# Whole 128x128 transposes for the half chunks of neighbourhood attention, in a one-core backbone step

## The chip, the cores and the metric

The kernel runs on one core of a Trainium2 chip. The metric is the device time of one execution in microseconds (us); the time of a kernel is the median of its runs.

## What is computed

One inference step of a hybrid backbone with one layer: 256 context tokens and 2048 latent tokens (a grid of 32 rows by 64 columns), 1024 wide, everything in float32. Each token is normalised and modulated, goes through one combined input projection into three mixers and their gates, and the mixers' outputs are merged, projected and added. What the change touches is the first mixer, attention with 8 heads of 64:

```python
s_loc = einsum(q_blk, k_band) * scale + bias      # latent: 8 x 16 neighbourhood, NEG_INF outside
s_ctx = einsum(q_blk, ctx_k) * scale              # and all 256 context keys
p = softmax(concatenate([s_loc, s_ctx], axis=-1), axis=-1)
o = einsum(p_loc, v_band) + einsum(p_ctx, ctx_v)
```

Context tokens attend to the 256 context keys alone. The other two mixers (a bidirectional gated linear recurrence and a short gated convolution) and the projections are untouched.

## The kernel before, in words

**Dense work and side work.** Most of the time goes into the input projection. `w_in_chunk` (lines 147 to 155) makes one tile of 128 output columns by 512 (or 256) tokens with 24 matmuls at line 153: each float32 operand is split into a high and a low part, and three products stand for one. Attention rides along: a generator (`Side`, line 181) is advanced by one or more units after each dense chunk, so that on TensorE units of attention stand between dense chunks. In the first attention stage (lines 819 to 824) one step goes with each dense chunk: first the prompt's 16 units, then the 32 units of latent group 0. In the second (lines 858 to 867) 101/27 steps, almost four, go with each of 28 dense chunks; these are the 96 units of the groups 1, 2 and 3.

**Groups, jobs, units.** The latent grid is cut into four groups of 8 rows, that is 512 queries (`GR`, line 697). A job is a group and a head; a unit is one of four blocks of 16 columns in it, 128 queries (8 rows by 16 columns) on the partitions. A unit's keys are 11, 15, 15 or 12 rows of 32 columns (352, 480, 480 or 384 keys) and the 256 context keys.

**One unit.** `attend1` (lines 575 to 599) computes scores on TensorE (line 583 against the context keys, line 587 against the neighbourhood, two products each) and the softmax on VectorE (DVE) and ScalarE (ACT): maximum at lines 588 and 590, negation at 595, exponential at 596, reciprocal at 597, scaling at 598. The result `p` has 128 query rows and up to 736 key columns. `attend2` (lines 601 to 616) transposes `p` in chunks of 128 keys, because the product with the values needs the keys on the partitions: line 611 on TensorE into PSUM banks `t`, then line 614 copies each bank to `pT` on ScalarE. `attend3` (lines 618 to 624) multiplies `pT` with the values, two units alternating, one in PSUM partitions 0 to 63 and one in 64 to 127. `advance` (line 635) keeps two units between `attend1` and `attend2`, and calls `attend3` for two units at a time (line 639), that is with every second unit.

**Half chunks.** A chunk holds 4 rows of keys. Some chunks lie within reach of only the upper or only the lower four query rows of the unit; lines 699 and 700 list for each group which chunk meets which queries. `(0, 0, 64)` says: chunk 0 for queries 0 to 63 alone. Groups 0 and 3 have one such half chunk in each unit, groups 1 and 2 have two, one for queries 0 to 63 and one for 64 to 127. Lines 777 to 779 spread the chunks of a unit, with the two chunks of context keys, over two banks: four whole chunks and one half for groups 0 and 3; three whole ones and a half, then one whole and a half, for groups 1 and 2. Before the change line 611 transposes of a half chunk only its 64 query rows, with the 64x64 corner of the identity; in the trace such a transpose has the shape `64*128 64x64`, a whole one `128*128 128x128`.

**Loads.** All of attention's loads are issued on GpSimd's (POOL's) queue: for each job the queries `qs` (line 728, 512 KB, both halves of the array hold a copy), the gate `sg` (line 734), for some the bias `bt` (line 731), for each new head its keys `kd` and `ck` (lines 715 and 717) and its values `vb` (line 722). The loads of the next job are issued after the first unit of a job (lines 785 to 788). `qs` has two buffers, so a load waits until the scores of the job two before have read theirs. POOL also computes the low parts of the weights (`wlo`, line 56). The dense weights `wraw` come on SP's queue.

Of the kernel before, what the change touches and what calls it, by code (L numbers as in the profile page):

```python
# [15 lines left out]
P = 128  # L16
# [28 lines left out]
def build(nc, tc, H):  # L45
    es = ExitStack()
    V, S, G, TE, SY = nc.vector, nc.scalar, nc.gpsimd, nc.tensor, nc.sync
# [46 lines left out]
    ident = cp.tile([P, P], F32, tag="ident", name="ident")  # L94
# [24 lines left out]
    def bank(name):  # L119
        return psA.tile([P, 512], F32, tag="bank", name=name, bufs=8)  # L120
# [115 lines left out]
    with tc.tile_pool(name="p0", bufs=2) as p0:  # L236
# [50 lines left out]
        w = p0.tile([P, 8], F32, tag="w", name="w", bufs=1)  # L287
# [313 lines left out]
    def attend2(nm, p, pv, oap):  # L601


        pT = AT[0].tile([P, 640], F32, tag="pT", name=f"pT{nm}", bufs=4)
        base, todo = 0, []
        for bi, part in enumerate(pv):
            tb = bank(f"t{bi}{nm}")
            off = 0
            for c0, v, keys, q0, q1 in part:
                w = q1 - q0  # L610
                TE.transpose(tb[:, off : off + w], p[q0:q1, c0 : c0 + P], ident[q0:q1, q0:q1])  # L611
                todo.append((oap(q0, q1), v[:keys], pT[:keys, base + off : base + off + w]))
                off += w
            S.copy(pT[:, base : base + off], tb[:, :off])  # L614
            base += off
        return todo

    def attend3(todos):

# [15 lines left out]
    def advance():  # L635
        if pend:
            old = pend.pop(0)
            tpd.append((attend2(*old[:4]), old[4]))
        if len(tpd) > 2 or (tpd and not pend):
            two = [tpd.pop(0) for _ in range(min(2, len(tpd)))]  # L640
            attend3([todo for todo, _ in two])
            for _, fin in two:
                if fin:
                    fin()
# [431 lines left out]
```

## Time and profile before

| what | value |
|---|---|
| time, median of 3 runs | 2610.14 us (2605.08 to 2614.53) |
| the profiled execution's own time | 2611.47 us |
| its span, first to last instruction | 2609.7 us |
| mean granted clock of TensorE (share of full speed) | 0.985 |
| TensorE matmuls busy | 2542.3 us (97%) |
| VectorE, ScalarE, GpSimd busy | 1104.2, 978.3, 876.7 us |
| instructions | 35312 |

How to read it: PE is TensorE's matmuls, PEld its weight loads, which overlap them; DVE is VectorE, ACT ScalarE, POOL GpSimd, SP the engine that issues most DMAs. An engine with a q behind it is its sequencer. L611 is line 611. A matmul is given as `out<-weights-side operands`, then the shape of the used array (rows*columns) and that of the moving operand; matmuls are pipelined, their ends are modelled and one starts before the last has ended. In a timeline a row is one or several instructions alike (x4): start in us from the span's beginning, duration in us, engine, line, operation, tiles, shape; in brackets the engine's idle time before it and what ended that. `issue` stands for idle time that no profiled event ended. In a group by shape the count is followed by busy us, the mean ns of one, and idle us before them. PEclk is the granted clock as a share of 2.4 GHz; a stretch is either at 1.0 (2.4 GHz) or at 0.5 (1.2 GHz), and other figures are means.

### The profile page before, as it was taken

The page shows a single profiled execution, that of the slowest core. Times are in us where ns is not written, and L with a number is a line of the kernel's source. Part 1 is how long each engine was busy: PE and PEld are TensorE (multiplying, and loading weights), DVE is VectorE, ACT ScalarE, POOL GpSimd, SP SyncE. Part 2 cuts the span into 40 slices and gives each one's busy share as a digit, 9 for nine tenths or more (in the row PEclk, how much of TensorE's full clock was granted, in tenths as well). Part 3 has the DMA queues.
Part 4 walks back from the last instruction along what each step waited for, and adds up shares of the span by engine and source line. Part 5 has one row for each costly group of instructions (what it writes and reads, how often), then busy time and mean ns, then how long its engine had stood idle before and what let it go on. Part 6 is the DMA issues. An engine that isn't in the chain of part 4 may idle for free.

```text
span 2609.7 us, 35312 instructions
## 1 busy us (share of the span) xinstructions
PE 2542.3 (97%) x13192; PEld 2077.4 (80%) x13192; DVE 1104.2 (42%) x2329; ACT 978.3 (37%) x1849; POOL 876.7 (34%) x757
## 2 busy tenths in 40 slices
PE   8999999999999999999999997999999999999998
PEld 4887788888878888888888886777777888888887
DVE  5101245555123331325777863455444134333433
ACT  4312443444223334436665653444444311111221
POOL 2311223323532321522544443233231413334642
PEclk9999999999999999999999998999899999999999
DMA  7335642332733434435642335455442466545442
GB/s 275 112 87 159 170 122 81 68 70 69 188 106 119 148 121 145 133 101 135 190 156 91 115 121 179 136 146 151 131 137 77 155 224 200 177 157 186 159 141 88
DMA packets 248812, 360.84 MB, mean 138 GB/s; under 512 B 88761, under 2 KB 124729, under 8 KB 247617
## 3 DMA queue, kind: packets, MB, share of 16 engines
q1 hardware_dynamic: 147360, 227.20, 28.7%
q0 software_dynamic: 47920, 64.26, 8.8%
q10 hardware_dynamic: 53360, 67.13, 7.8%
q8 instruction: 104, 1.70, 0.3%
q14 instruction: 68, 0.55, 0.1%
HBM read 248.10 MB, written 110.11 MB: 137 GB/s over the span
## 4 chain that ended last, share of the span: by engine, by line
PE 75%; DMA 6%; issue 4%; POOL 2%; DVE 1%; ACT 0%; SPq 0%; ACTq 0%; POOLq 0%; DVEq 0%
PE ps L153 45%; PE pb L932 12%; PE po L981 8%; DMA qs<-d_q 3%; PE t L611 3%; PE o L624 2%; PE pg L454 2%; PE pv L321 1%; PE sl L587 1%; PE sc L583 1%; DMA bt<-bias 1%; DMA d_z<-sp 1%; POOL wlo L56 0%; DMA kp<-d_k 0%; DMA d_q<-evl 0%
## 5 line engine op out<-in xcount | busy, mean ns | idle before, releaser
L153 PE MATMUL ps<-xh,whi 128*128 128x512 f32 (+1 forms) x2400 | 899.6, 375 | 0.0
L153 PE MATMUL ps<-xl,whi 128*128 128x512 f32 (+1 forms) x2400 | 888.8, 370 | 2.4 <-DVE xl L56 1.6
L153 PE MATMUL ps<-xh,wlo 128*128 128x512 f32 (+1 forms) x2400 | 888.2, 370 | 0.0
L153 PEld LDWEIGHTS ps<-xh,whi 128*128 128x128 f32 x2400 | 455.2, 190 | 93.7 <-issue 6.2
L56 POOL TENSOR_TENSOR wlo<-wraw,whi 128x512 fp32r<-128x512 f32 x240 | 334.0, 1409 | 570.0 <-ACT whi L55 505.3
L153 PEld LDWEIGHTS ps<-xh,wlo 128*128 128x128 f32 x2400 | 455.1, 190 | 78.1
L153 PEld LDWEIGHTS ps<-xl,whi 128*128 128x128 f32 x2400 | 455.2, 190 | 77.8 <-POOL xl L56 2.0
L55 ACT CAST whi<-wraw 128x512 fp32r<-128x512 f32 x240 | 144.8, 616 | 300.1 <-PE ps L153 160.9
L932 PE MATMUL pb<-zh,wbh 128*128 128x512 f32 (+1 forms) x480 | 179.0, 373 | 4.3 <-ACT zh L55 4.3
L167 ACT ACTIVATE evm<-ps 128x512 f32<-128x512 f32 (+1 forms) x120 | 66.3, 552 | 301.1 <-PE ps L153 300.2
L932 PE MATMUL pb<-zl,wbh 128*128 128x512 f32 (+1 forms) x480 | 179.1, 373 | 0.0
L932 PE MATMUL pb<-zh,wbl 128*128 128x512 f32 (+1 forms) x480 | 179.0, 373 | 0.0
L588 DVE TENSOR_SCALAR_CACHE_REDUCE p<-sc 128x256 f32<-128x256 f32 x127 | 53.9, 424 | 254.1 <-PE sc L583 253.1
L939 POOL TENSOR_TENSOR tg<-tg,tg 128x512 f32<-128x512 f32 (+1 forms) x80 | 96.9, 1221 | 188.5 <-DVE tg L935 184.3
L935 DVE SCALAR_TENSOR_TENSOR tg<-tg,pb 128x512 f32<-128x512 f32 (+1 forms) x120 | 74.7, 631 | 151.8 <-PE pb L932 139.8
L611 PE MATMUL t<-ident,p 128*128 128x128 f32 (+1 forms) x698 | 129.4, 286 | 7.0 <-DVE ast L595 3.4
L611 PEld LDWEIGHTS t<-ident,p 128*128 128x128 f32 (+1 forms) x698 | 91.6, 142 | 53.9 <-issue 19.6
L614 ACT COPY pT<-t 128x512 f32<-128x512 f32 (+3 forms) x256 | 96.2, 406 | 75.0 <-PE t L611 74.7
L596 ACT ACTIVATE p<-p,ast 128x736 f32<-128x736 f32 (+2 forms) x127 | 109.4, 862 | 39.5 <-DVE ast L595 38.1
L444 DVE SCALAR_TENSOR_TENSOR uf<-ut,pk,uf 128x512 f32<-128x512 f32 (+1 forms) x120 | 103.0, 858 | 30.5 <-ACT uf L441 28.6
L475 POOL TENSOR_TENSOR sq<-sq,ea 128x512 f32<-128x512 f32 (+1 forms) x40 | 61.9, 1548 | 154.2 <-ACT sq L468 92.6
L55 ACT CAST zh<-zr 128x512 fp32r<-128x512 f32 (+1 forms) x60 | 30.5, 575 | 211.8 <-PE pb L932 92.6
(233 smaller groups left out, 3689.7 us busy)
## 6 DMA issues: line engine op xcount, KB each, us to landing
wraw<-w_in SPq DMA_DIRECT2D x240, 256.0 KB, 3.4
d_sig<-evm ACTq DMA_DIRECT2D x96, 256.0 KB, 3.5
tg<-d_sig SPq DMA_DIRECT2D x96, 256.0 KB, 3.8
xt<-x SPq DMA_DIRECT2D x36, 512.0 KB, 3.7
qs<-d_q POOLq DMA_DIRECT2D x32, 512.0 KB, 17.1
zr<-d_z SPq DMA_DIRECT2D x12, 1024.0 KB, 5.4
d_mrg<-tg ACTq DMA_DIRECT2D x32, 256.0 KB, 4.4
mr<-d_mrg SPq DMA_DIRECT2D x8, 1024.0 KB, 5.8
```

Source lines behind the costliest of these rows:

```text
L55: S.copy(hi, src)
L56: lo_eng.tensor_tensor(lo, src, r2f(hi), ALU.subtract)
L153: TE.matmul(ps[:, :n], (lo if a else hi)[:, k, :], (xl if b else xh)[ci][:, k, :], start=(i == 0), stop=(i == len(ps_) - 1))
L167: S.activation(o[:, :n], ps, AF.Tanh, scale=0.5)
L444: V.scalar_tensor_tensor(uf[:, :n], ut[:, tap : tap + n], cw(tap), uf[:, :n], ALU.mult, ALU.add)
L596: S.activation(p[:, :nk], p[:, :nk], AF.Exp, bias=st[:, 2:3], accum_out=st[:, 3:4])
L611: TE.transpose(tb[:, off : off + w], p[q0:q1, c0 : c0 + P], ident[q0:q1, q0:q1])
L614: S.copy(pT[:, base : base + off], tb[:, :off])
L932: TE.matmul(ps[:, :n], (wbl if a_ else wbh)[br * 4 + k][:, m * P : (m + 1) * P], (zl if b_ else zh)[:, k, :n], start=(i == 0), stop=(i == ...
L935: V.scalar_tensor_tensor(t[:, :n], t[:, :n], 1.0, ps[:, :n], ALU.add, ALU.mult)
L939: G.tensor_tensor(acc[m][:, :n], acc[m][:, :n], t[:, :n], ALU.add)
L981: TE.matmul(ps, (ml if a_ else mh)[:, k, j * P : (j + 1) * P], (wol if b_ else woh)[k][:, hs], start=(i == 0), stop=(i == len(ps_) - 1))
```

## The change

`attend2` transposes each chunk whole, half chunks too: all 128 rows of `p` with the whole identity, into 128 columns of the bank. Of a half chunk only the 64 columns that belong to its queries are used. So that these lie together with the others, the chunks of a bank are sorted: a half for queries 64 to 127 comes first, a half for queries 0 to 63 last, whole ones between, and the copy of line 614 takes the columns from `first` to `last`, as many as before, though the unused half stands before or behind them. In the banks of the kernel this moves one chunk, the second half of groups 1 and 2, ahead of the whole chunk beside it. The products with the values keep their operands; the returned list is sorted so that those of 64 queries come last, which again concerns groups 1 and 2 alone.

```diff
@@ -605,15 +605,19 @@
         base, todo = 0, []
         for bi, part in enumerate(pv):
             tb = bank(f"t{bi}{nm}")
-            off = 0
-            for c0, v, keys, q0, q1 in part:
-                w = q1 - q0
-                TE.transpose(tb[:, off : off + w], p[q0:q1, c0 : c0 + P], ident[q0:q1, q0:q1])
-                todo.append((oap(q0, q1), v[:keys], pT[:keys, base + off : base + off + w]))
-                off += w
-            S.copy(pT[:, base : base + off], tb[:, :off])
-            base += off
-        return todo
+
+
+            part = sorted(part, key=lambda x: (x[3] == 0) + (x[4] < P))
+            first = part[0][3]
+            for ti, (c0, v, keys, q0, q1) in enumerate(part):
+                TE.transpose(tb[:, ti * P : ti * P + P], p[:, c0 : c0 + P], ident)
+                col = base + ti * P + q0 - first
+                todo.append((oap(q0, q1), v[:keys], pT[:keys, col : col + q1 - q0]))
+            last = (len(part) - 1) * P + part[-1][4]
+            S.copy(pT[:, base : base + last - first], tb[:, first:last])
+            base += last - first
+
+        return sorted(todo, key=lambda x: x[2].shape[-1] < P)
```

## Rows read from the trace of the kernel before

**Rows 1.** The page: busy time by engine; then the chain that ended last.
```profile
PE 2542.3 (97%) x13192; PEld 2077.4 (80%) x13192; DVE 1104.2 (42%) x2329; ACT 978.3 (37%) x1849; POOL 876.7 (34%) x757
...
PE ps L153 45%; PE pb L932 12%; PE po L981 8%; DMA qs<-d_q 3%; PE t L611 3%; PE o L624 2%; PE pg L454 2%; PE pv L321 1%; PE sl L587 1%; PE sc L583 1%; DMA bt<-bias 1%; DMA d_z<-sp 1%; POOL wlo L56 0%; DMA kp<-d_k 0%; DMA d_q<-evl 0%
```

**Rows 2.** Windows: length, busy (count) per engine, granted clock, DMA share, GB/s.
```profile
core 0: us, PE busy (x) PEld busy (x) DVE busy (x) ACT busy (x) POOL busy (x), PEclk, DMA share, GB/s
690.00:1000.00 310.00, 304.24 (x1902) 258.31 (x1901) 94.03 (x330) 105.72 (x255) 96.11 (x93) 0.99 0.41 126
1000.00:1560.00 560.00, 559.91 (x2554) 465.14 (x2551) 335.69 (x433) 306.98 (x459) 224.59 (x159) 1.00 0.43 133
1560.00:2032.00 472.00, 437.21 (x2804) 343.53 (x2803) 212.65 (x730) 202.29 (x462) 135.25 (x124) 0.94 0.47 137
```

**Rows 3.** Groups by shape, PE, line 611: count, busy us, mean ns, idle.
```profile
L611 PE MATMUL t<-ident,p 128*128 128x128 f32 x508 | 94.0, 288 | 7.0 <-DVE ast L595 3.4 <-DVE p L598 3.4
...
L611 PE MATMUL t<-ident,p 64*128 64x64 f32 x190 | 52.9, 279 | 0.0
```

**Rows 4.** Timelines (start, us): a half chunk among whole ones, then dense.
```profile
867.67 0.60 PE L611 MATMUL t<-ident,p 128*128 128x128 f32 x4
...
868.20 0.14 PEld L611 LDWEIGHTS t<-ident,p 64*128 64x128 f32 x1 [0.17 <-DVE p L588]
...
868.40 0.38 PE L153 MATMUL ps<-xh,whi 128*128 128x256 f32 x1
868.62 0.28 PE L153 MATMUL ps<-xl,whi 128*128 128x256 f32 x1
```

**Rows 5.** Timeline, PE: two whole chunks, then dense matmuls; two, then line 624.
```profile
789.84 0.38 PE L611 MATMUL t0p<-ident,pp 128*128 128x128 f32 x2
...
790.18 0.28 PE L153 MATMUL ps<-xl,whi 128*128 128x256 f32 x1
...
719.90 0.38 PE L611 MATMUL t0p<-ident,pp 128*128 128x128 f32 x2
720.21 0.33 PE L624 MATMUL op<-pTp,vpr 128*64 128x128 f32 x2
```

**Rows 6.** Timeline, PEld: a half chunk, then line 624.
```profile
1703.38 0.13 PEld L611 LDWEIGHTS t<-ident,p 64*128 64x128 f32 x1 [0.17 <-issue]
1703.58 0.14 PEld L624 LDWEIGHTS o<-pT,vb 128*64 128x64 f32 x2
```

**Rows 7.** Timeline, PE: a middle group's six chunks.
```profile
1747.59 1.15 PE L611 MATMUL t<-ident,p 128*128 128x128 f32 x6
```

**Rows 8.** Waits of PE, 1560 to 2032 us: total us, times, longest.
```profile
PE sc L583 <- DMA qs<-d_q: 20.5, 6, 9.0
PE t L611 <- DVE ast L597: 4.1, 1, 4.1
PE t L611 <- DVE ast L595: 3.4, 4, 1.7
PE t L611 <- DVE p L598: 3.4, 8, 1.6
```

**Rows 9.** Timelines, PE and POOL: a query load, its release, its reader.
```profile
1911.73 0.53 PE L587 MATMUL sl<-kd,qs 128*128 128x384 f32 x2
...
1912.75 2.10 POOL L728 DMA_DIRECT2D qs<-d_q  x1
...
1931.91 0.36 PE L583 MATMUL sc<-ck,qs 128*128 128x256 f32 x1 [2.79 <-DMA qs<-d_q]
```

**Rows 10.** The page, DMA issues: count, KB each, median us to landing.
```profile
qs<-d_q POOLq DMA_DIRECT2D x32, 512.0 KB, 17.1
```

**Rows 11.** Timelines: first and last of 24 query loads, last job's start.
```profile
1577.75 2.11 POOL L728 DMA_DIRECT2D qs<-d_q  x1
...
1979.62 2.12 POOL L728 DMA_DIRECT2D qs<-d_q  x1 [0.90 <-PE sl L587]
...
1998.86 0.38 PE L583 MATMUL sc<-ck,qs 128*128 128x256 f32 x1
```

## Prediction

> **What bounds the kernel now.** I read the page first: TensorE is busy 97% of the span, and the chain that ended last runs over its lines; the one transfer with a visible share of that chain is the query load `qs<-d_q`, 3% [rows 1]. Then the windows, because a share of the whole span hides stages: from 690 to 1000 us (group 0 and the prompt) PE is busy 304 of 310 us and from 1000 to 1560 us all the time, but from 1560 to 2032 us (groups 1 to 3) only 437 of 472 us, and there the granted clock falls to 0.94 [rows 2]. So a microsecond taken from PE in the first attention stage is a microsecond of the end, and the dense stage behind it passes it on; in the second attention stage it must first be asked what PE waits for.
>
> Then the transposes of line 611 by shape: a half chunk (64 rows, 64 columns of identity) takes as long as a whole one in the record, 279 against 288 ns [rows 3]. The record of one instruction therefore doesn't tell the price; the distance between starts does. Four whole chunks that last 0.60 us together, each 0.27, start 0.11 us apart, so the fourth starts at 868.00. The half chunk behind it starts at 868.20 and what follows at 868.40: 0.20 us on both sides, with the weight load idle for 0.17 us before the half [rows 4]. The same 0.20 stands between two whole chunks and line 624, whose weights are 64 columns wide [rows 5]. What these places share is a change of the used rows or columns of the array: each change costs about a tenth of a microsecond more than going on in one form.
>
> **The change part by part.** There are 192 half chunks: one in each of the 64 units of groups 0 and 3 and two in each of the 64 units of groups 1 and 2 (the table shows 190 of them; the other two bear the name of the stage's first tile [rows 3]). Each becomes a whole one.
>
> 1. Entry into the half: 0.20 becomes the 0.11 between two whole chunks, 0.095 us saved [rows 4].
> 2. Way out of it. (a) Into a whole chunk, once in each unit of groups 1 and 2: 0.20 becomes 0.11, 0.094 saved. (b) Into dense matmuls or the next unit's scores, which use all 128 rows too: the first starts 0.20 us after a half but nearly at once after a whole, so I take the second. From 868.20 to 868.62 it is 0.42 us after a half [rows 4]; after two whole chunks, the second of which starts at 789.95, it comes at 790.18, 0.23 later [rows 5]: 0.19 saved. (c) Into line 624: 0.20 after a half [rows 6] and 0.20 after a whole (720.01 to 720.21, [rows 5]), nothing saved. Line 639 lets line 624 run after every second unit, so half of the units leave by (c).
>
> A unit with two halves fits this: its six transposes take 1.15 us, where six whole ones would take 5 x 0.11 + 0.27 = 0.82 [rows 7]; the steps above, without the way out, make 0.28.
>
> 3. Stage one has 32 halves: 32 x 0.095 + 16 x 0.19 = 6 us. Stage two has 160 in 96 units: 160 x 0.095 + 64 x 0.094 + 48 x 0.19 = 30 us at full clock. The mean clock of 0.94 [rows 2] means that PE spends about an eighth of that stage at its lower level, where the same steps take longer, so I put 34 us (an estimate; between 30 and 38).
>
> 4. The copies of line 614 read and write as many columns as before, from another offset, and four chunks of 128 columns fill a bank's 512. ScalarE waits for the last transpose of a bank, which now comes earlier. The sort at the end puts 64-column products last; their number and widths don't change. Nothing for all of these, between -1 and +1 us.
>
> **What takes some of it back.** Stage two has 24 jobs (a head and a group, four units each) in some 420 us, about 17.4 us apart, and each needs a query load of 512 KB that takes 17.1 us from issue to landing [rows 10]. There are two buffers: the load for a job goes out when the last score matmul of the job two before has read its buffer. Followed once: that matmul's pair starts at 1911.73, POOL issues at 1912.75, and the first score that reads it, at 1931.91, has kept PE idle for 2.79 us [rows 9]. Six such waits make 20.5 us, of which 9.0 is the stage's first load [rows 8]. A faster PE frees the buffer only as much earlier as it has gained so far; the 15 to 20 us of flight stay.
>
> I therefore rolled the 24 loads forward (the first goes out at 1577.75, the last at 1979.62 [rows 11]): a job starts at the later of (start of the job before + its own PE stretch, less 1.7 us for groups 1 and 2 or 0.85 for group 3) and (landing of its load, moved earlier by as much as the release two jobs back). The waits for landings, 14.7 us without the stage's first, grow to 27, and the last job starts 19.6 us earlier; with its own saving that makes 20 of the 34. With every flight 1 us longer the same sum gives 12, with 3 us shorter the whole 34 and a little more.
>
> DVE and ScalarE work two units ahead of the transposes. PE waits 10.9 us for them in this stage now (4.1 + 3.4 + 3.4, [rows 8]); with a third of a microsecond less per unit on PE, such waits become longer. And a long wait of PE may bring more of the lower clock. Both together I put at 3 us, between 0 and 11 (those waits doubled). No load, store or queue order is changed in the code: POOL issues the same loads behind the same releases, and SP and ScalarE's queue the same transfers.
>
> The sum: 6 + 20 - 3 = 23 us, from the profiled execution's 2611.5 us (span 2609.7): 2588.5. That execution lies 1.3 us above the median of the runs shown (2610.1), so against the median I say 2587.
>
> **A rule against it.** By the starts measured here the step into a half takes 0.20 us and the step into a whole 0.11 [rows 4]. The Trainium skill (TensorE: Matmul & The Clock Gate, section Back-to-back issue gap) gives a spacing of about 60 cycles for up to 64 moving columns and 134 for 128. By that table alone each whole chunk would be 74 cycles dearer and the change would lose about 6 us, an estimate from that page. The trace disagrees where halves stand among whole ones: there the narrow one costs more, not less.
>
> **The rivals.** (A) The loads bind stage two throughout: its 34 us all become waits for `qs`, and only stage one's 6 us are left: 2604. For it: the jobs' distance and the flight time are nearly equal, and 1 us more of flight takes 8 us of the gain. Against it: nine of the 24 jobs find their load landed 4 us or more before; the last one, issued at 1979.62, is first read at 1998.86, 19.2 us later [rows 11]. Chance 0.13.
>
> (B) The loads don't bind: the flights shorten, or the waits fall where PE had to wait anyway. Then 6 + 34 = 40 us: 2570. For it: the slack just named; against it: six waits for these loads stand there already [rows 8]. Chance 0.14.
>
> (C) Slower: the 0.20 us around a half comes not from the change of form but from what stays there, such as the semaphore or the bank, and the 64 added columns are paid on top. By [rows 4] 128 columns take 0.11 us, so 64 more cost 0.054 us at most: 192 x 0.054 = 10 us, 2621. It decides if a whole chunk in a former half's place still starts 0.20 us after its forerunner. Against it: whole chunks lead into dense work without such a gap [rows 5], and in groups 1 and 2 one half stands in the middle. Chance 0.06. If the gaps stay and the columns cost nothing, the change does not do what it says and the time stays at 2610; that hundredth or two is counted under (A), whose band it shares.
>
> **How the numbers follow.** My own case has 0.67. Its range is 2577 to 2597: 30 to 38 us of price, a flight 1 us longer or shorter, 0 to 11 us for DVE, ScalarE and the clock. Reaching to (B) and most of (A) gives 2570 to 2604; left out are (C) and part of (A). A measurement here tells about 0.3%, 8 us, from no change. Faster by more: my case and (B), 0.81. Within it: (A), 0.13. Slower: (C), 0.06.
>
> **What would show it.** In the profile after: line 611 has no shape of 64 rows; six transposes of a unit of groups 1 and 2 take 0.82 us, not 1.15; the idle 0.17 us before a half's weight load is gone; the first attention stage is 6 us shorter. In the second, the scores' wait for `qs` rises from 20.5 to about 33 us, in more places than six. I am wrong if the 0.20 stays with whole chunks (C), if the waits for `qs` rise by the whole saving (A) or not at all (B), or if the waits for DVE's `p` and `ast` rise beyond 20 us, which would make another engine the bound there.

## The result, and the profile after

The changed kernel takes 2581.5 us (median; 2576.9 to 2583.9) where the kernel before takes 2610.9: ratio 0.9887, interval 0.9869 to 0.9905, that is 25 to 34 us, about 29. The forecast was 2587 us, 23 us less.

The page of the changed kernel: its span, the engines' busy time, the query loads.

```profile
span 2575.0 us, 35310 instructions
...
PE 2492.4 (97%) x13192; PEld 2059.2 (80%) x13192; DVE 1104.6 (43%) x2329; ACT 976.4 (38%) x1849; POOL 876.9 (34%) x757
...
qs<-d_q POOLq DMA_DIRECT2D x32, 512.0 KB, 17.5
```

The same 13192 matmuls fill 50 us less of busy time than in [rows 1]: none was removed, they stand closer together, and the mean granted clock of the execution is 0.990 instead of 0.985. The query loads take about as long as before, 17.5 us against 17.1 [rows 10].

Where the time went is read from the starts of the transposes. In the view of one line (count, shortest/median/longest ns, first and last start in us), the kernel before has these two rows; the second, `p_first`, marks the start of the second attention stage:

```profile
L611 PE MATMUL t<-ident,p x698: 271/272/477, 793.5 to 2022.8; 128*128 128x128 f32 x159, 64*128 64x64 f32 x16
...
L611 PEld LDWEIGHTS t<-ident,p_first x6: 178/182/230, 1606.5 to 1608.0; 128*128 128x128 f32 x4, 64*128 64x128 f32 x2
```

and the changed kernel, whose line 613 is the former line 611:

```profile
L613 PE MATMUL t<-ident,p x698: 270/272/473, 793.8 to 1987.0; 128*128 128x128 f32 x175
...
L613 PEld LDWEIGHTS t<-ident,p_first x6: 183/231/231, 1600.6 to 1601.5; 128*128 128x128 f32 x6
```

The first transposes of group 0 start at the same time (793.5 and 793.8). At `p_first` the changed kernel is 5.9 us ahead (1606.5 and 1600.6): that is stage one (with the first load of the second, whose wait of some 9 us lies ahead of `p_first` in both). From there to the last transpose it is 416.3 us before and 386.4 after: 29.9 us for stage two. The rest, about a microsecond, is given back in the last stages: spans of 2609.7 and 2575.0 are 34.7 apart. This profiled execution is the fastest of its four, so the stages here sum to more than the medians' 29.

Line 611's shapes, as in [rows 3], and one unit of a middle group, as in [rows 7]:

```profile
L613 PE MATMUL t<-ident,p 128*128 128x128 f32 x698 | 100.5, 279 | 10.3 <-DVE p L598 8.1 <-DVE ast L595 2.1
```

```profile
1703.43 0.82 PE L613 MATMUL t<-ident,p 128*128 128x128 f32 x6
```

No shape of 64 rows is left, and six transposes take the forecast 0.82 us, not 1.15. The whole chunk's mean of 279 ns is no shorter than the half's was: as before, the price is not in the record of one instruction.

The window of stage two, with the columns of [rows 2], bounded so that it holds about the same attention work:

```profile
1555.00:2000.00 445.00, 396.65 (x2815) 329.29 (x2815) 211.77 (x731) 201.53 (x463) 137.69 (x126) 0.97 0.50 146
```

Stage two has the granted clock at 0.97 instead of 0.94 in these two executions (how far two of them differ is taken up below). And PE's waits in it, as in [rows 8]:

```profile
PE sc L583 <- DMA qs<-d_q: 29.2, 11, 9.5
PE t L613 <- DVE p L598: 8.1, 10, 2.1
PE t L613 <- DVE ast L597: 3.5, 1, 3.5
...
PE t L613 <- DVE ast L595: 2.1, 2, 1.6
```

The wait for the query loads has grown from 20.5 us in 6 places to 29.2 in 11, and the waits for DVE's `p` and `ast` (the rows of line 613) from 10.9 to 13.7. All of PE's waits in the stage together, with those of the scores for other things, go from 34.6 us to 48.2.

### The profile page after: what moved, and what is told of

It is laid out like the page before. It is cut to its first block, busy times and chain, and to the rows that moved or that the text cites. A ratio compares the mean times of both kernels' runs of the same rounds, so it can differ in the third digit from the quotient of the medians.

```text
span 2575.0 us, 35310 instructions
## 1 busy us (share of the span) xinstructions
PE 2492.4 (97%) x13192; PEld 2059.2 (80%) x13192; DVE 1104.6 (43%) x2329; ACT 976.4 (38%) x1849; POOL 876.9 (34%) x757
## 5 line engine op out<-in xcount | busy, mean ns | idle before, releaser
L613 PE MATMUL t<-ident,p 128*128 128x128 f32 x698 | 100.5, 279 | 10.3 <-DVE p L598 8.1
L936 PEld LDWEIGHTS pb<-zh,wbh 128*128 128x128 f32 x480 | 91.4, 191 | 22.1 <-ACT zh L55 4.7
## 6 DMA issues: line engine op xcount, KB each, us to landing
qs<-d_q POOLq DMA_DIRECT2D x32, 512.0 KB, 17.5
```

Of the source, the lines that this page charges most:

```text
L613: TE.transpose(tb[:, ti * P : ti * P + P], p[:, c0 : c0 + P], ident)
L936: TE.matmul(ps[:, :n], (wbl if a_ else wbh)[br * 4 + k][:, m * P : (m + 1) * P], (zl if b_ else zh)[:, k, :n], start=(i == 0), stop=(i == ...
```

## The experiments

Each gives the median of its runs and the ratio to the kernel before on the same chip.

**The two half chunks of a unit put side by side.** In the kernel before:

```diff
-                pv = [fu[:3] + hv[:1], fu[3:] + hv[1:]] if len(hv) == 2 else [fu, hv]
+                pv = [fu[:3] + hv[:1], hv[1:] + fu[3:]] if len(hv) == 2 else [fu, hv]
```

> The kernel before, with only the second bank's order of groups 1 and 2 turned round: the half chunk of the lower queries comes ahead of the whole chunk, so that the two half chunks of a unit follow one another (whole, whole, whole, half, half, whole). The number of halves, their rows and columns are as before. Theory 1 (the price is the change of form): one entry of 0.095 us and one way out are saved in each of 64 units, 64 x (0.095 + half of 0.19) = 12 us on TensorE, of which the loads of the second stage take about half: 2603 to 2606 us; the step from half to half is 0.11 us or less. Theory 2 (each half pays 0.20 us on its own account, whatever stands beside it): the step from half to half is 0.20 us and the time stays at 2611.

Measured: 2601.3 us against 2613.5, ratio 0.9948 (0.9933 to 0.9963), 10 to 17 us faster. The timelines of PE and, in a window that holds the two half chunks, PEld:

```profile
1739.95 0.95 PE L611 MATMUL t<-ident,p 128*128 128x128 f32 x6
```

```profile
1740.37 0.14 PEld L611 LDWEIGHTS t<-ident,p 64*128 64x128 f32 x2 [0.17 <-issue]
```

The weights of both half chunks, one in the upper and one in the lower 64 rows, are loaded within the 0.14 us that one of them takes, and the six transposes take 0.95 us instead of the 1.15 of [rows 7]. As many halves as before, of the same shape, are cheaper by 0.20 us in a unit when one change of form less stands beside them. By the trace the second half starts 0.003 us after the first. Theory 2, a price that each half pays whatever stands beside it, is refuted: a half right behind another pays nothing. The price goes with the change of form: the 0.20 us between whole chunks and line 624 [rows 5] have no half in them. The gain is larger than the 6 to 8 us expected, which is taken up below. The Trainium skill (TensorEngine Tiling (Array Packing), section Key Properties) says that changing the tiling mode, not just the tile, drains the engine, and that different tiles can load weights and multiply in parallel: both statements agree with this run, 0.17 us of idle weight loading ahead of the first half and none between the two.

**Three buffers for the queries**, in the kernel before and in the changed one:

```diff
-            qs = at.tile([P, 2, 512], F32R, tag="qs", name=f"qs{g}_{h}")
+            qs = at.tile([P, 2, 512], F32R, tag="qs", name=f"qs{g}_{h}", bufs=3 if g else 2)
```

> The kernel before with a third buffer for the queries in the second attention stage, so that a load can go out one job earlier. Theory 1 (a load's flight binds the stage): the scores' waits for the query load fall from 20.5 us to the first one's 9, and with them the stretches of lower clock behind such waits; 10 to 18 us faster, 2593 to 2601. Rival (the waits only show a stage that is bound by something else): the waits move to other tiles and the time stays within 3 us of 2611.

> The changed kernel with the same third buffer. Theory 1: its waits for the query load, 29.2 us, fall to about 9, and the time to 2557 to 2565, so that the distance to the kernel before with three buffers is the whole price of the forms, 34 to 40 us. Rival A (another engine binds once the loads don't): waits for DVE's p and ast rise from 14 to over 25 us and the distance stays at 29 or less. Theory 3 (the gain of the second stage is mostly the clock, which fell behind long waits): with no waits in either kernel the granted clock is the same in both and the distance shrinks to 30, the price of the forms at full clock with stage one's 6 us counted in.

Measured: 2590.7 us, ratio 0.9904 (0.9876 to 0.9932), and 2560.0, ratio 0.9781 (0.9755 to 0.9808). The distance between the two is 30.7 us, about that without the third buffer. PE's waits in stage two, first the kernel before with three buffers, then the changed one:

```profile
PE sc L583 <- DMA qs<-d_q: 8.6, 1, 8.6
PE t L611 <- DVE ast L595: 5.3, 4, 2.3
PE t L611 <- DVE p L598: 4.5, 8, 2.4
PE t L611 <- DVE p_first L598: 2.8, 1, 2.8
PE t L611 <- DVE ast L597: 1.6, 1, 1.6
```

```profile
PE t L613 <- DVE p L598: 13.3, 8, 3.7
PE sc L583 <- DMA qs<-d_q: 8.6, 1, 8.6
PE t L613 <- DVE ast L595: 3.0, 3, 1.7
PE t L613 <- DVE p_first L598: 2.4, 1, 2.4
```

The only query load still waited for is the stage's first, so the loads did hold TensorE, in both kernels. The kernel before gains 23 to 25 us (by medians and by ratio), more than the 10 to 18 expected, from a buffer that removes 12 us of waits: the granted clock of its execution rises too, from 0.986 (median of the runs of before) to 0.991, and 0.005 of 2610 us are 13 us (an estimate). The rival that the waits only stood for another limit is refuted. But the distance doesn't grow to the 34 to 40 us of theory 1: what PE no longer waits for loads it partly waits for DVE, 18.7 us in all against 14.2 in the kernel before with three buffers, most of it for `p` of line 598. That is 4.5 us of the difference; the rest isn't placed, and runs of one kernel spread by 5 to 8 us here. Rival A's mark (over 25 us of DVE waits) isn't reached; its direction is right. The clock is the same in both (0.991 and 0.990), and the distance is 30.7, where theory 3 put 30; so this pair alone can't tell theory 3 from rival A. The next pair does.

**Two transfers for each query load**, in the changed kernel and in the kernel before:

```diff
-            G.dma_start(r2f(qs), twice(h, 256 + 512 * g, 512))
+            for a in (0, 1):
+                G.dma_start(r2f(qs[a * HD : a * HD + HD]), d_q[rows(h), :, 256 + 512 * g : 768 + 512 * g])
```

> The changed kernel with each query load of the latent groups issued as two transfers, one for each half of the partitions, in place of one transfer that reads the queries twice. Two buffers as before. If the one transfer's flight of 17 us comes from how it is cut into packets, the two land within 5 to 8 us, the waits for them go, and the time is that of three buffers, 2557 to 2565; POOL issues 24 more transfers of some 0.6 us, which it has room for. If the flight comes from the amount of data or from the queue ahead, it stays at 15 us or more and the time at 2581.

> The kernel before, half chunks as they were, with each latent query load as two transfers. Theory 1 (192 half chunks cost their changes of form, and nothing of that can hide once no load is waited for): 33 to 37 us above the changed kernel with two transfers (2532), that is 2565 to 2569, with a granted clock of about 0.995 as there. Theory 4 (half chunks also bring the lower clock, whatever PE waits for): the clock stays at 0.991 or less, more than 10 us of lower clock stand in the second attention stage, and the distance is over 40, 2573 or more. Theory 5 (the changed kernel's loads only took the gain because of the flight, and DVE takes it once they are gone): distance under 28.

Measured: 2532.3 us, ratio 0.9681 (0.9655 to 0.9708), and 2571.6, ratio 0.9827 (0.9808 to 0.9845). The ratios are 0.0146 apart, 38 us of 2611, good to some 8 us by their intervals; the medians, on two chips, are 39.3 apart. The DMA issues of the changed kernel with two transfers (count, KB each, median us to landing):

```profile
qs<-d_q POOLq DMA_DIRECT2D x64, 256.0 KB, 5.9
```

A load lands 5.9 us after its issue instead of 17.5. The changed kernel's 2532 us are 25 us below the 2557 to 2565 expected, which were the time with three buffers. That more than the waits for `qs` would go was not foreseen: the stage's first wait, 8.6 us with three buffers, is gone too; the other loads on POOL's queue land sooner (the keys `kd` of 896 KB in 8.1 us instead of 19.1, the biases in 6.3 to 7.4 instead of 16.0 to 17.5); and the granted clock is 0.995 instead of 0.990. The transposes and PE's waits of stage two, first in the changed kernel, then in the kernel before, both with two transfers:

```profile
L613 PE MATMUL t<-ident,p x698: 270/273/331, 795.2 to 1942.5; 128*128 128x128 f32 x175
...
L613 PEld LDWEIGHTS t<-ident,p_first x6: 137/141/144, 1589.5 to 1590.0; 128*128 128x128 f32 x6
```

```profile
PE t L613 <- DVE p L598: 9.5, 10, 2.5
PE t L613 <- DVE p_first L598: 2.4, 1, 2.4
PE t L613 <- DVE ast L595: 1.4, 2, 0.7
```

```profile
L611 PE MATMUL t<-ident,p x698: 271/272/477, 797.4 to 1983.0; 128*128 128x128 f32 x159, 64*128 64x64 f32 x16
...
L611 PEld LDWEIGHTS t<-ident,p_first x6: 134/138/142, 1598.4 to 1599.4; 128*128 128x128 f32 x4, 64*128 64x128 f32 x2
```

```profile
PE t L611 <- DVE p L598: 3.5, 9, 1.6
PE t L611 <- DVE ast L595: 3.3, 4, 1.5
PE t L611 <- DVE p_first L598: 2.5, 1, 2.5
```

No score waits for a query load any more, in either. From `p_first` to the last transpose it is 353.0 us with whole chunks and 384.6 with halves: 31.6 less, in spite of 4.0 us more of waits for DVE (13.3 against 9.3). So TensorE itself saves about 35.6 us in stage two, where the forecast had 30 at full clock and 34 in all. The granted clock of both executions is 0.995. Theory 4 is refuted: half chunks don't bring the lower clock by themselves. Theory 5 is too, and theory 3: at the same clock TensorE alone saves those 35.6 us in stage two, and the distance is 38, not 30. Theory 1 put 33 to 37 us; 38 to 39 are measured, which agrees within the 8 us.

**The prompt's query loads too as two transfers**, on top, in the changed kernel:

```diff
-            G.dma_start(r2f(qp), twice(h, 0, 256))
+            for a in (0, 1):
+                G.dma_start(r2f(qp[a * HD : a * HD + HD]), d_q[rows(h), :, 0:256])
```

> The changed kernel with two transfers for each query load, the prompt's included. If the prompt's scores wait for keys that stand behind a query load on POOL's queue, 3 to 6 us less than with the latent ones alone: 2526 to 2529. If they wait for the release of their buffers, 2532.

Measured: 2524.1 us, ratio 0.9645 (0.9627 to 0.9662), the fastest version here, 93 us below the kernel before on its chip. By the ratios that is 9 us less than with the latent loads alone, good to some 8, where 3 to 6 were expected. PE's waits for the prompt's keys, `kp`, from 690 to 1000 us, with the latent loads alone cut in two and then with all:

```profile
PE scp L583 <- DMA kp<-d_k: 5.2, 2, 5.0
```

```profile
PE scp L583 <- DMA kp<-d_k: 0.3, 1, 0.3
```

The keys did stand behind a query load on POOL's queue: 5.2 us of waits become 0.3.

**The changed kernel once more.**

> The changed kernel as it is, beside the others on this chip. From the first measurement: ratio 0.985 to 0.991. Its granted clock against that of the kernel before in these runs tells how much of the gain the clock gave: theory 1 with the loads taking 10 us of 36 and the clock returning 5 to 8 wants the clock 0.002 to 0.004 above that of before; if the clock is the same, the loads took less than the profile's longer waits say.

Measured: 2585.1 us, ratio 0.9880 (0.9861 to 0.9898), 27 to 36 us. The median granted clock of its runs is 0.988; that of the kernel before in these runs and in those above is 0.986. Its transposes:

```profile
L613 PE MATMUL t<-ident,p x698: 270/272/421, 799.9 to 1995.4; 128*128 128x128 f32 x175
...
L613 PEld LDWEIGHTS t<-ident,p_first x6: 182/230/230, 1607.8 to 1608.7; 128*128 128x128 f32 x6
```

Stage two takes 387.6 us from `p_first` to the last transpose, within 1.2 us of the first execution's 386.4. The clock is 0.002 above that of the kernel before, at the lower end of what theory 1 wanted.

**Whole transposes in group 0 alone.** `attend2` takes the new loop for the units of group 0 and the prompt and the old one for the others; the list of products isn't sorted.

```diff
+            if "_0_" not in nm[1:]:
+                off = 0
+                for c0, v, keys, q0, q1 in part:
...
+                S.copy(pT[:, base : base + off], tb[:, :off])
+                base += off
+                continue
```

> Whole transposes in group 0 alone, the units of the first attention stage; groups 1 to 3 as before. Theory 1 (TensorE bounds that stage and the dense stage behind it passes the gain on): 6 us faster than before, ratio 0.9977, and the second stage as long as before. Rival (the gain is lost before the end, for instance in the first load of the second stage): no change.

Measured: 2607.0 us, ratio 0.9964 (0.9948 to 0.9981), 5 to 14 us faster. The forecast 6 us lie in that interval and no change doesn't. Its transposes, whose line is 612 here for groups 1 to 3 and 621 for group 0:

```profile
L612 PE MATMUL t<-ident,p x538: 271/272/476, 1613.2 to 2010.0; 128*128 128x128 f32 x130, 64*128 64x64 f32 x50
...
L612 PEld LDWEIGHTS t<-ident,p_first x6: 178/183/230, 1603.6 to 1605.1; 128*128 128x128 f32 x4, 64*128 64x128 f32 x2
...
L621 PE MATMUL t<-ident,p x160: 271/272/273, 796.5 to 994.6; 128*128 128x128 f32 x160
```

From the first transposes of group 0 to `p_first` it is 807.1 us, against 813.0 in the kernel before and 806.8 and 807.9 in the two executions of the changed kernel. Stage two, of which nothing was changed, takes 406.4 us here against 416.3 in the profile of before. That is how far two executions of the same instructions lie apart where a stage hangs on loads and on the clock; single profiles of this stage are good to some 10 us, and only the ratios to less.

## Why the prediction was right, and which term was off

**What bounds what: right.** TensorE's starts, not its records, gave the price, and the gain came out at the end. Stage one gave 5.9 us of the forecast 6, and for that change alone the forecast total lies within the measured interval.

**Steps 1 and 2, entry and way out: right, with one row read and not used.** Whole chunks follow each other at 0.11 us in the changed kernel (the median of its starts), and halves stood at 0.20 from what was beside them. The sentence under [rows 7] noted that the six transposes exceeded the even pace by 0.33 us and the steps made 0.28, called that a fit, and went on with 0.28. The missing 0.05 is real. It lies in the step into the second half of a unit, shown here by the weight loads of the unit of [rows 7], which stand for half, whole, half:

```profile
1748.01 0.60 PEld L611 LDWEIGHTS t<-ident,p 64*128 64x128 f32 x3 [0.17 <-issue]
```

The last of the three lasts 0.14 us, so it starts 0.46 after the first: 0.20 to the whole chunk and 0.26, not 0.20, from there to the second half. In 64 units that is 3 us more, and with it step 3's 30 us at full clock come to 33 or 34. By the median starts in the two traces (0.20, 0.26 and 0.20 beside a half, 0.11 between whole chunks, 0.03 from a whole chunk into dense work or scores) the change is worth 39 us in both stages together, which is what the two-transfer pair shows; the stage-two part measured there is about 36, 33 by these starts. The 34 us that the forecast put down were thus nearly right, but by luck: an uplift for the lower clock stood in for a step that was too small. The same holds for the expectation of the experiment with halves side by side: by the starts in its trace a unit saves 0.29 us on average, way out included, 18 us in 64 units and not 12, of which 12 to 14 arrived.

**Step 4, copies and order of products: right, nothing.** With two transfers the steps alone add up to the measured distance, and no loss is left to place there.

**What takes some of it back: the mechanism right, the size too large, and this is the term that made the forecast 6 us too small.** Without waits for loads the change is worth 38 to 39 us; with two buffers and the 17 us flight it is worth 29 to 31 (the ratios of the first measurement and the repetition, each good to some 5 us). So 7 to 10 are taken back, where the forecast took 17: 14 for the loads and 3 for DVE and the clock. By parts, in the two profiles: the wait for `qs` was to rise to about 33 us and rose to 29.2, nearly as rolled forward; the waits for DVE were to cost up to 11 us and grew by 2.8. What had the wrong sign is the clock. The forecast let longer waits bring more of the lower level; they didn't: the mean clock of a run is 0.988 to 0.989 (medians of the first measurement and the repetition) instead of 0.986. At 2600 us, 0.0025 of clock are 6.5 us (an estimate), about the size of the miss. The profiles of stage two alone don't show this so clearly: against the 0.94 and 0.97 above, the same stage has 0.96 with half chunks in the run with whole transposes in group 0 alone, and 0.96 with whole ones in the repetition.

**Why the clock didn't fall further stays open.** Half chunks alone don't lower it (0.995 with halves and no waits for loads). Waits go with a lower one: the kernel before goes from 0.986 to 0.991 with a third buffer. But the changed kernel has longer waits and a slightly higher clock than the kernel before, and no run here separates how the two work together.

**The rivals.** (A), the loads take all of stage two, is refuted by the 29 us; (B), they take nothing, by the 38 to 39 that appear when they can't; (C), the gap stays with the place and the columns are paid on top, by the 0.82 us of six whole chunks and by the halves side by side. The table of the Trainium skill (TensorE: Matmul & The Clock Gate, section Back-to-back issue gap) that the prediction set against itself, by which whole chunks would have lost 6 us, fails here as the trace had said: it counts columns and leaves out what stands between two forms.

## What to carry to other kernels

Price a small TensorE instruction by the distance between starts, with its neighbours, and look at what changes between them: here a step into or out of a half took 0.20 us where 0.11 or 0.03 stand between whole ones, 192 halves cost 38 to 39 us, and the wider instruction was the cheaper one. Where a sum of steps falls short of a row that holds them all, as 0.28 of 0.33 did, take the row. And when a faster engine will wait for a load, look at the load's own flight first: cutting it into two transfers was worth some 50 us more in the changed kernel (ratios of 0.9887 and 0.9681) and 45 in the kernel before, more than the change studied.

## What the runs showed that was not expected

**A transfer that reads the same data twice.** One transfer of 512 KB whose outermost step goes over two copies of the queries takes 17.5 us; two of 256 KB, each with 64 partitions outermost, take 5.9, on the same queue. The Trainium skill (DMA: Bandwidth & Descriptors, section Rules for kernel authors) says that an outermost dimension of a size below 16, such as a leading broadcast of c copies, confines a transfer to c engines at most. The traces agree as far as they go (which engines took part isn't in them). The packets on POOL's queue, first in the changed kernel, then with two transfers:

```profile
q0 software_dynamic: 47920, 64.26, 9.0%
...
q0 software_dynamic: 19760, 64.03, 8.9%
```

And by the packets' times, two of that queue's packets and no more are under way at once for 5.6 us in the 20 us behind such an issue (median), and for 0.3 us with two transfers, where 16 at once is the commonest number while any are.

**Two half transposes at once.** The upper and the lower half load their weights in the time of one when they are neighbours (above). Whole chunks are still better: 0.82 us against 0.95 for a unit.

**DVE stretched while POOL issues.** In the kernel before, POOL's issue of a query load, DVE's scaling of `p` in that time, and the transposes behind it:

```profile
1751.83 2.11 POOL L728 DMA_DIRECT2D qs<-d_q  x1
```

```profile
1752.13 2.09 DVE L598 TENSOR_SCALAR p<-p,ast 128x640 f32<-128x640 f32 x1
```

```profile
1754.28 0.55 PE L611 MATMUL t<-ident,p 128*128 128x128 f32 x3 [1.69 <-DVE ast L595]
```

Line 598 takes 2.09 us there for a tile that takes 0.55 elsewhere (1742.69 us, the same shape), and it ends 0.3 us after the issue does; PE has stood idle for 1.69 us by then, waiting for DVE. Whether the issue causes it wasn't tried; in the same stage three more such stretches begin inside the issue of a query load, and three don't. Those three stand beside POOL's `wlo` of line 56 (at 1604.13, 1653.80 and 1918.03 us). Nor does every issue bring one: of the 18 scalings in the whole trace that begin inside an issue of a query load, ten take about 1.2 us or more.
